# Turned units, early fourth sums, and causal masks added by VectorE, in the hybrid encoder layer on one core

## The chip, the cores and the metric

The kernel runs on one core of a Trainium2 chip. The metric is the time of one execution in device microseconds; several runs of a kernel are taken, and the median counts. Matmuls run on TensorE (PE in the profile, its weight loads PEld) and write to banks of PSUM; VectorE (DVE) and ScalarE (ACT) do the elementwise work; SyncE (SP) and GpSimd (POOL) only issue transfers here.

## The reference

One layer for 512 tokens of width 2048, in float32. A normed input goes through one wide projection into three token mixers of four heads each (width 128), their gates, and three merge gates; the mixers' outputs are projected up, weighted by the gates, summed, projected again and added to the input.

```python
hn = rmsnorm(x, norm_g)
proj = jnp.einsum('bsd,dc->bsc', hn, w_in)     # q, k, v, gate of A, B, C; merge gates
...
# A: logits + c[query] - c[key]; mask = key <= query; softmax; @ v
# B: logits + a bias by relative distance; softmax over the last 9 chunks of 64; @ v
# C: z = q.k * scale; mask = key < query; lk = where(mask, log_sigmoid(-z), 0)
#    a = where(mask, exp(z + sums of lk over later keys), 0); @ v
ys = ys * jax.nn.silu(br[:, :, :, 3])
up = jnp.einsum('bsnw,nwd->bsnd', ys, w_up)
merged = jnp.sum(gates * up, axis=2)
return x + jnp.einsum('bsd,de->bse', merged, w_out)
```

A and C are causal, so their scores need a mask in the 128x128 block on the diagonal of each block of 128 queries.

## The kernel before, in words

**Precision.** Every operand of a large matmul is split into a high part (rounded to the type that TensorE runs fast) and a low part, the rest. ScalarE writes the high part (L245), VectorE subtracts it from the source for the low part (L249). A product is high x high, high x low and low x high. The inputs' two parts lie side by side, 256 tokens each, so that one matmul of 512 columns does weights' high part times both (tile `wh`), and one of 256 columns does weights' low part (tile `wl`) times the inputs' high part.

**Products.** Two columns of 128 outputs each, over a depth of 2048 and two halves of the tokens, are computed by Strassen's scheme with seven products instead of eight (class `PairTask`). A unit (class `Pair`) is one such product: eight matmuls of 512 with `wh` and then eight of 256 with `wl`, into one PSUM bank. The units of a pair come in the order 1, 2, 6, 5, 7, 3, 4; products 6, 7, 3 and 4 go on adding onto the bank of an earlier one (6 onto 1, 7 onto 6, 3 onto 5, 4 onto 7). Sums of weights are made by GpSimd's adding transfers and by VectorE (L631, L637), sums of inputs by `combos`.

**Stages.** First four columns of C's head 0 directly; then, for each of the other heads, its q and k, v and gate as pairs of columns, with the columns of the merge gates between; then the up stage, where for each of 16 blocks of 128 output rows (row block d) three mixers' outputs `y` are multiplied with `w_up` (36 matmuls of 512 columns) and weighted by gates loaded from DRAM into `sg` tiles; then the output projection with `w_out`, again in pairs. `merged_a` and `merged_b` make the sums of inputs that the output's products read: `m1`, `m2`, `m23` (second and third sums) and `m4` (the fourth sums, products 4). Row blocks k and k + 8 make the sums of index k. The fourth sum is written into a tile `mu`, kept, and split into its two parts only when the up stage is over (`late_t4`). The first output pair works in the order 1, 5, 2, 3, 6, 7, 4 with 256-wide matmuls throughout (`late`).

**Attention.** Each head's scores, transposes and value products are spread by `stages` over the units of the next heads. `soft_scores` (A and B) does three matmuls (L259 to L261) for a block of queries i and all keys up to it, then VectorE adds the bias and takes the maximum in one instruction (L986). For A a fourth matmul, the identity times the mask table in bfloat16, adds the mask (L981); `stick_scores` (C) does the same (L1037) before ScalarE copies the scores to `z` (L1042).

**What sets the order.** The program is recorded by a planner, class `Flow`: tasks are generators that yield what they wait for (an event, a number of free buffers in a `Slots` pool) or an engine with an estimated cost, and the one that can start first goes next, by its due time where two can. `stream` walks through the list of units; `at(u, g)` spawns a task when unit u is reached. The order that comes out is fixed on TensorE, ScalarE and VectorE. `t2s` counts the 20 work buffers of 128x512, `atts` four PSUM banks for attention and the up stage, `accs` four for products, `xps` the tiles that hold inputs in two parts, `raws` the buffers for weights as loaded.

Of the kernel before, what the change touches and what calls it, by code (L numbers as in the profile page):

```python
# [15 lines left out]
P = 128  # L16
# [9 lines left out]
UK = 8  # L26
# [122 lines left out]
def mm_us(n, x=1):  # L149
    return x * max(0.115, n / 2400 + 0.0133)  # L150
# [11 lines left out]
def hybrid_kernel(  # L162
# [151 lines left out]
    identb = cp.tile([P, P], BF16, name="identb")  # L314
    nc.vector.tensor_copy(identb, identf)

# [32 lines left out]
    def at(u, g):  # L349
        side.setdefault(u, []).append(g)  # L350

    class Unit:


        def __init__(self, mms, after=None, shape=(UK, P), srcs=()):
            self.shape, self.mms, self.after, self.srcs = list(shape), mms, after, srcs
            self.ready_hi, self.ready, self.there, self.raw = Event(), Event(), Event(), None

# [229 lines left out]
    class PairTask:  # L588
# [57 lines left out]
        def mms_of(self, i):  # L646
            p = self.order[i]
            bank = (0, 1, 2, 0, 0, 1, 2)[i] if self.late else {2: 1, 5: 2, 3: 2}.get(p, 0)
            onto = None if self.late else {6: 1, 7: 6, 4: 7, 3: 5}.get(p)
            more = onto is not None  # L650
            single = self.late or self.plain_end and p == 4
# [3 lines left out]
            def go(u):  # L655
                if more:
# [6 lines left out]
                for j in range(UK):  # L663
                    yield lambda: self.ops[p](j) is not None
                    r, _, ev = self.ops[p](j)
                    yield ev
                    if single:
                        yield PE, mm_us(HS)
                        mm(self.ps[p][:, LH], u.hi[:, j, :], r[:, 0, :], j == 0 and not more, more=more)
                    else:  # L670
                        yield PE, mm_us(S)
                        mm(two(self.ps[p]), u.hi[:, j, :], r, j == 0 and not more, more=more)
                    if single:
                        yield PE, mm_us(HS)
                        mm(self.ps[p][:, LH], u.hi[:, j, :], r[:, 1, :], more=more)
                yield u.ready
                for j in range(UK):
                    yield PE, mm_us(HS)
                    mm(self.ps[p][:, LH], u.lo[:, j, :], self.ops[p](j)[1], stop=j == UK - 1, more=more)
# [191 lines left out]
    class Head:  # L871
# [98 lines left out]
        def soft_scores(self, i):  # L970
# [6 lines left out]
            yield PE, mm_us(m, 3) + (0.05 if n == A else 0)  # L977
# [11 lines left out]
            give(atts)  # L989
            yield ACT, act_us(m) + 0.25  # L990
# [35 lines left out]
        def stick_scores(self, i):  # L1026
# [7 lines left out]
            yield PE, mm_us(m, 3) + 0.05  # L1034
            ps = att()[:, :m]
            mm3(ps, qh[:, blk(i)], ql[:, blk(i)], kh[:, :m], kl[:, :m], True, False)
            nc.tensor.matmul(ps[:, blk(i)], identb, mskc, start=False, stop=True)  # L1037
# [5 lines left out]
            give(atts)  # L1043
            yield t2s, 2
# [89 lines left out]
        def stages(self):  # L1134
# [118 lines left out]
    def schedule(head, a, b):  # L1253
        for (d, g), base in [(g, a) for g in head.stages()[0]] + [(g, b) for g in head.stages()[1]]:
            at(base + d, g)
# [131 lines left out]
    m1, m2, m23, m4 = [None] * UK, [None] * UK, [None] * UK, [None] * (UK // 2)  # L1387
    m4_ev = [Event() for _ in range(UK // 2)]
    kept_m, m1_ev, mus, up_half, up_done = {}, [Event() for _ in range(UK)], {}, Event(), Event()
# [9 lines left out]
    def merged_b(k, b):  # L1399
# [4 lines left out]
        if k % 2 == 0:  # L1404
            yield t2s, 1
            mus[k // 2] = t2("mu")
        u = mus[k // 2][:, RH if k % 2 else LH]
# [11 lines left out]
        minus(u, t[:, LH], b[:, LH])  # L1419
        give(t2s)  # L1420
        ready = up_half if k < 5 else up_done
# [7 lines left out]
        yield up_done  # L1429
        yield from late_t4(k, u, due)  # L1430

    def late_t4(k, u, due):
        if k % 2 == 0:
            yield xps, 1
            m4[k // 2] = Parts("m4")
            set_(m4_ev[k // 2])
        yield m4_ev[k // 2]
        h, lo, ev = m4[k // 2].half(k % 2)
        yield from split(h, lo, u, HS, ev, (due + 14.0,))
        if k % 2:  # L1440
            give(t2s)
# [10 lines left out]
    mops = strassen_ops(m1, m2, m23, m4)  # L1452
# [76 lines left out]
    def stream():  # L1529
        for i, u in enumerate(units):  # L1530
            cur[0] = i
            for g in side.pop(i, ()):
                spawn(g(), 5.0, flow.fin)
# [3 lines left out]
            yield u.ready_hi  # L1537
            yield from u.mms(u)
# [20 lines left out]
KEPT = 1  # L1559
WARM = 16  # L1560
# [59 lines left out]
```

## Time and profile before

| | |
|---|---|
| median of 3 runs | 1327.93 us (1326.29 to 1328.51) |
| the profiled execution | 1328.65 us |
| its span in the trace | 1326.9 us |
| granted TensorE clock | 1.0 |
| busy | PE 1320.2, DVE 1134.7, ACT 805.9, POOL 94.9 us |

A page of the profile has busy time by engine first, the chain of work that ended last in its part 4, and groups of instructions by source line in its part 5. Views of the trace give waits (who waited for whom: us in total, times, longest), windows (busy time by engine in a stretch), and the timeline (start, length, engine, line, operation, tiles written and read, size, count; in brackets idle time of the engine before it and what ended it). Matmuls overlap, so the distance from one start to the next is the time that one holds the array. Many operations are recorded by helpers: L264 is every matmul of a product, L245 and L249 every split.

### The profile page before, as it was taken

The page shows a single profiled execution, that of the slowest core. Times are in us where ns is not written, and L with a number is a line of the kernel's source. Part 1 is how long each engine was busy: PE and PEld are TensorE (multiplying, and loading weights), DVE is VectorE, ACT ScalarE, POOL GpSimd, SP SyncE. Part 2 cuts the span into 40 slices and gives each one's busy share as a digit, 9 for nine tenths or more (in the row PEclk, how much of TensorE's full clock was granted, in tenths as well). Part 3 has the DMA queues.
Part 4 walks back from the last instruction along what each step waited for, and adds up shares of the span by engine and source line. Part 5 has one row for each costly group of instructions (what it writes and reads, how often), then busy time and mean ns, then how long its engine had stood idle before and what let it go on. Part 6 is the DMA issues. An engine that isn't in the chain of part 4 may idle for free.

```text
span 1326.9 us, 20238 instructions
## 1 busy us (share of the span) xinstructions
PE 1320.2 (99%) x7506; PEld 1150.5 (87%) x7506; DVE 1134.7 (86%) x1676; ACT 805.9 (61%) x1280; POOL 94.9 (7%) x120
## 2 busy tenths in 40 slices
PE   9999999999999999999999999999999999999998
PEld 6898888888888888888888888888888888888887
DVE  8989888788888889888898979888898877897786
ACT  8767657575556665666656665666557655454443
POOL 0000001000010100000000000000000000001000
PEclk9999999999999999999999999999999999999999
DMA  9776776767786776867878777776779755668893
GB/s 336 207 206 168 190 198 176 212 177 190 200 203 172 197 201 181 219 160 207 200 182 215 173 193 201 192 196 181 194 178 272 278 194 184 193 172 243 235 254 94
DMA packets 89651, 266.24 MB, mean 201 GB/s; under 512 B 10560, under 2 KB 12608, under 8 KB 89552
## 3 DMA queue, kind: packets, MB, share of 16 engines
q1 hardware_dynamic: 70400, 203.86, 46.4%
q0 software_dynamic: 15552, 56.63, 25.8%
q10 hardware_dynamic: 3600, 4.46, 0.9%
q8 instruction: 59, 0.97, 0.3%
q14 instruction: 40, 0.33, 0.1%
HBM read 245.21 MB, written 19.70 MB: 200 GB/s over the span
## 4 chain that ended last, share of the span: by engine, by line
PE 98%; DVE 1%; DMA 0%; issue 0%; DVEq 0%
PE acc L264 84%; PE att L264 8%; PE att L1008 1%; PE att L259 1%; PE att L260 1%; PE att L1121 1%; PE att L1122 1%; PE att L261 1%; PE att L1120 1%; PE att L1072 0%; PE att L1222 0%; DMA begin_in<-in_begin 0%; PE att L909 0%; PE att L910 0%; DVE m L249 0%; DVE wl L249 0%
## 5 line engine op out<-in xcount | busy, mean ns | idle before, releaser
L249 DVE TENSOR_TENSOR wl<-raw,wh 128x1024 fp32r<-128x1024 f32 (+2 forms) x418 | 499.8, 1199 | 141.9 <-ACT wh L245 133.6
L245 ACT ACTIVATE wh<-raw 128x1024 fp32r<-128x1024 f32 (+2 forms) x418 | 434.1, 1039 | 145.3 <-PE acc L264 62.3
L264 PE MATMUL acc<-x,wh 128*128 128x512 f32 (+1 forms) x1568 | 399.2, 391 | 0.7 <-DVE gq L333 0.7
L264 PEld LDWEIGHTS acc<-x,wh 128*128 128x128 f32 x1568 | 277.3, 189 | 50.1 <-issue 2.2
L264 PE MATMUL acc<-t,wh 128*128 128x512 f32 (+1 forms) x1128 | 283.7, 390 | 0.0
L264 PEld LDWEIGHTS acc<-t,wh 128*128 128x128 f32 x1128 | 198.1, 189 | 32.9
L264 PEld LDWEIGHTS acc<-x,wl 128*128 128x128 f32 x1504 | 207.0, 190 | 17.2 <-DVE x L441 0.8
L264 PE MATMUL acc<-x,wl 128*128 128x256 f32 (+1 forms) x1504 | 216.8, 285 | 0.0
L264 PEld LDWEIGHTS acc<-t,wl 128*128 128x128 f32 x1104 | 151.6, 190 | 11.4
L264 PE MATMUL acc<-t,wl 128*128 128x256 f32 x1104 | 155.5, 282 | 0.0
L282 POOL DMA_DIRECT2D raw<-in_w_col x92 | 79.5, 864 | 924.1 <-DMA raw<-in_w_col 573.8
L264 PE MATMUL acc<-m,wh 128*128 128x512 f32 (+1 forms) x512 | 113.7, 366 | 1.5 <-DVE m L249 1.5
L264 PEld LDWEIGHTS acc<-m,wh 128*128 128x128 f32 x512 | 85.4, 190 | 14.4 <-DVE m L249 1.9
L815 ACT ACTIVATE c<-acc 128x256 f32<-128x256 f32 x51 | 19.6, 383 | 97.1 <-PE acc L264 94.1
L782 ACT ACTIVATE u<-acc 128x512 f32<-128x512 f32 x51 | 30.3, 594 | 79.4 <-PE acc L264 79.4
L761 ACT ACTIVATE u<-acc 128x512 f32<-128x512 f32 x52 | 31.1, 598 | 71.9 <-PE acc L264 70.8
L637 DVE TENSOR_TENSOR raw<-raw,raw 128x1024 f32<-128x1024 f32 x54 | 65.9, 1220 | 0.5
L631 DVE TENSOR_TENSOR raw<-raw,raw 128x1024 f32<-128x1024 f32 x54 | 65.8, 1219 | 0.4
L264 PE MATMUL att<-y,wh 128*128 128x512 f32 x256 | 65.8, 389 | 0.0
L264 PEld LDWEIGHTS acc<-m,wl 128*128 128x128 f32 x448 | 60.6, 191 | 3.7
L264 PE MATMUL acc<-m,wl 128*128 128x256 f32 x448 | 62.5, 282 | 0.0
L264 PEld LDWEIGHTS att<-y,wh 128*128 128x128 f32 x256 | 48.0, 188 | 10.0
(207 smaller groups left out, 1397.2 us busy)
## 6 DMA issues: line engine op xcount, KB each, us to landing
raw<-in_w_col SPq DMA_DIRECT2D x230, 512.0 KB, 4.5
raw<-in_w_col POOLq DMA_DIRECT2D x92, 512.0 KB, 6.4
raw<-in_w_out SPq DMA_DIRECT2D x40, 512.0 KB, 5.3
gl<-c SPq DMA_DIRECT2D x48, 256.0 KB, 3.5
raw<-in_w_up SPq DMA_DIRECT2D x32, 384.0 KB, 3.6
sg<-gl SPq DMA_DIRECT2D x48, 256.0 KB, 4.8
raw<-in_w_out POOLq DMA_DIRECT2D x16, 512.0 KB, 6.9
xn<-in_xn SPq DMA_DIRECT2D x16, 256.0 KB, 3.1
```

The costliest lines, as they stand in the source:

```text
L245: nc.scalar.activation(hi, src, AF.Copy)
L249: nc.vector.tensor_sub(lo, src, f(hi))
L259: nc.tensor.matmul(ps, lh, rh, start=start, stop=False, skip_group_check=more)
L260: nc.tensor.matmul(ps, lh, rl, start=False, stop=False, skip_group_check=more)
L261: nc.tensor.matmul(ps, ll, rh, start=False, stop=stop, skip_group_check=more)
L264: nc.tensor.matmul(ps, w, x, start=start, stop=stop, skip_group_check=more)
L282: nc.gpsimd.dma_start(to, src, accum_op=ALU.add)
L631: nc.vector.tensor_add(w[1], w[1], w[5])
L637: nc.vector.tensor_add(w[2], w[2], w[1])
L761: nc.scalar.activation(self.u, ps, AF.Copy)
L782: nc.scalar.activation(self.s, ps, AF.Copy)
L815: nc.scalar.activation(c, ps[:, RH], AF.Copy, scale=-1.0)
```

## The change

It has four parts. **Turned units:** a `Pair` that adds onto an earlier product's bank may run its low-part matmuls first and its high-part ones after; `stream` turns it when the unit before ended with low parts and the planner has its low part ready 0.4 us ahead. **Masks:** the matmuls with the mask tables go. For A, VectorE adds the mask into the diagonal block of the bias tile, in place; as a later block of queries needs that stretch of the bias without a mask, the blocks go from the last to the first, and the addition of block i waits for the maximum of block i + 1 (event "m"). For C, VectorE adds the mask to `z` after ScalarE's copy. **Fourth sums:** they are written into the upper half of `b`, split at once in the up stage, and kept in tiles `m4` out of the 20 work buffers `t2s` instead of in four tiles of `xps`; `m23` may take its tile one index earlier (k < 6). **Due times:** the sums of weights are due 1.5 us after they can start instead of 3, the last head's stages 3 instead of 5.

```diff
     class Pair(Unit):
+            self.single = task.late or task.plain_end and self.p == 4
+            self.onto = None if task.late else {6: 1, 7: 6, 4: 7, 3: 5}.get(self.p)
...
-                spawn(self.task.sums(), 3.0)
+                spawn(self.task.sums(), 1.5)
...
+                def high(first):
+                    for j in range(UK):
...
+                            mm(two(self.ps[p]), u.hi[:, j, :], r, start, stop, more)
+                def low(first):
+                    yield u.ready
+                    for j in range(UK):
...
+                        mm(self.ps[p][:, LH], u.lo[:, j, :], x, first and j == 0 and not more,
+                           not first and j == UK - 1, more)
+                steps = (low, high) if u.low_first else (high, low)
+                for first, step in zip((True, False), steps):
+                    yield from step(first)
...
     def soft_scores(self, i):
-            mm3(ps, qh[:, blk(i)], ql[:, blk(i)], kh[:, :m], kl[:, :m], True, n == B)
+            mm3(ps, qh[:, blk(i)], ql[:, blk(i)], kh[:, :m], kl[:, :m], True, True)
+            p = self.p[i]
             if n == A:
-                nc.tensor.matmul(ps[:, blk(i)], identb, mska, start=False, stop=True)
-            p = self.p[i]
+                if i < QB - 1:
+                    yield self.event("m", i + 1)
+                yield DVE, dve_us(P)
+                nc.vector.tensor_add(self.bias[:, blk(i)], self.bias[:, blk(i)], mska)
...
+            set_(self.event("m", i))
...
     def stick_scores(self, i):
-            mm3(ps, qh[:, blk(i)], ql[:, blk(i)], kh[:, :m], kl[:, :m], True, False)
-            nc.tensor.matmul(ps[:, blk(i)], identb, mskc, start=False, stop=True)
+            mm3(ps, qh[:, blk(i)], ql[:, blk(i)], kh[:, :m], kl[:, :m], True, True)
...
+            yield DVE, dve_us(P)
+            nc.vector.tensor_add(z[:, blk(i)], z[:, blk(i)], mskc)
...
-                g += [(s + i, one(self.soft_scores, i)) for i in range(QB)]
+                g += [(s + i, one(self.soft_scores, QB - 1 - i if self.n == A else i)) for i in range(QB)]
...
     def merged_b(k, b):
-        minus(u, t[:, LH], b[:, LH])
+        minus(b[:, RH], t[:, LH], b[:, LH])
+        yield t2s, 1
+        parts, ev = t2("m4", F32R), Event()
+        yield from split(parts[:, LH], parts[:, RH], b[:, RH], HS, ev)
         give(t2s)
-        ready = up_half if k < 5 else up_done
+        m4[k] = two(parts), parts[:, LH], ev
+        ready = up_half if k < 6 else up_done
...
-        yield up_done
-        yield from late_t4(k, u, due)
-
-    def late_t4(k, u, due):
...
     def stream():
+            if isinstance(u, Pair) and not u.single:
+                low_there = u.ready.t is not None and u.ready.t + AHEAD <= flow.clock[PE]
+                u.low_first = ends_low and u.onto is not None and low_there
+                ends_low = not u.low_first
+            else:
+                ends_low = False
...
+AHEAD = 0.4
```

Where instructions move, first on TensorE, at the third and fourth unit of a pair while a head of B is under way (`acc_4250` and `acc_4198` before are `acc_4248` and `acc_4195` in the changed kernel; `x` and `t` are inputs and their sums). Before:

```order
L264 MATMUL acc_4250<-x_17_130,wh_4173 128x512
L264 MATMUL acc_4250<-x_10_123,wl_4174 128x256
...
L264 MATMUL acc_4250<-x_17_130,wl_4174 128x256
L264 MATMUL acc_4198<-t_67_387,wh_4196 128x512
...
L264 MATMUL acc_4198<-t_102_644,wh_4196 128x512
L264 MATMUL acc_4198<-t_67_387,wl_4197 128x256
...
L264 MATMUL acc_4198<-t_102_644,wl_4197 128x256
L264 MATMUL acc_4314<-x_2_115,wh_4248 128x512
```

In the changed kernel:

```order
L264 MATMUL acc_4248<-x_17_128,wh_4171 128x512
L264 MATMUL acc_4248<-x_10_121,wl_4172 128x256
...
L264 MATMUL acc_4248<-x_17_128,wl_4172 128x256
L264 MATMUL acc_4195<-t_67_385,wl_4194 128x256
...
L264 MATMUL acc_4195<-t_102_642,wl_4194 128x256
L264 MATMUL acc_4195<-t_67_385,wh_4193 128x512
...
L264 MATMUL acc_4195<-t_102_642,wh_4193 128x512
L264 MATMUL acc_4312<-x_2_113,wh_4246 128x512
```

The eight `wl` matmuls of the later unit moved ahead of its eight `wh` ones, so two narrow runs stand together and then two wide ones. This is so in 136 units.

On VectorE, at the scores of A's first head (`cb` is the bias, `mx` the maxima). Before:

```order
L986 ISA p_7598,mx_7690<-att_7685,cb_7521 128x128
L988 TENSOR_SCALAR mx_7690<-mx_7690 128x1
L249 TENSOR_TENSOR wl_7663<-raw_7526,wh_7662 128x1024
L986 ISA p_7599,mx_7697<-att_7692,cb_7521 128x256
L988 TENSOR_SCALAR mx_7697<-mx_7697 128x1
...
L249 TENSOR_TENSOR wl_7720<-raw_7413,wh_7719 128x1024
```

In the changed kernel:

```order
L995 TENSOR_TENSOR cb_7519<-cb_7519,mska 128x128
L999 ISA p_7595,mx_7727<-att_7695,cb_7519 128x512
L1001 TENSOR_SCALAR mx_7727<-mx_7727 128x1
L779 TENSOR_TENSOR u_7683<-u_7683,acc_7686 128x512
L711 TENSOR_TENSOR c_1366_7744<-u_7683 128x256
L249 TENSOR_TENSOR wl_7736<-raw_7568,wh_7735 128x1024
L995 TENSOR_TENSOR cb_7519<-cb_7519,mska 128x128
...
L999 ISA p_7596,mx_7766<-att_7701,cb_7519 128x384
L1001 TENSOR_SCALAR mx_7766<-mx_7766 128x1
```

An addition into the bias stands ahead of each block's maximum, the widest block comes first, and low parts stand between.

On VectorE, at the first output pair (the numbers of `m23` tell its tiles apart). Before:

```order
L717 TENSOR_TENSOR c1_2181_12063<-u_2170_11987,acc_2178_12027 128x256
L249 TENSOR_TENSOR wl_2177_12026<-raw_2120_11720,wh_2176_12025 128x1024
L249 TENSOR_TENSOR m23_2157_11911<-mt_2082_11535,m23_2157_11911 128x2x256
L249 TENSOR_TENSOR m23_2163_11946<-mt_2110_11677,m23_2163_11946 128x2x256
L249 TENSOR_TENSOR m23_2164_11947<-mt_2137_11818,m23_2164_11947 128x2x256
L722 TENSOR_TENSOR c1_2181_12063<-c2_2175_12024,acc_2184_12066 128x256
L249 TENSOR_TENSOR m23_2174_12010<-mt_2166_11963,m23_2174_12010 128x2x256
...
L249 TENSOR_TENSOR m4_2165_11949<-mu_1973_10970,m4_2165_11949 128x256 x2
```

In the changed kernel:

```order
L249 TENSOR_TENSOR m4_2180_12057<-sg_2134_11807,m4_2180_12057 128x256
L727 TENSOR_TENSOR c1_2182_12073<-u_2170_11997,acc_2179_12036 128x256
L249 TENSOR_TENSOR wl_2172_11999<-raw_2127_11764,wh_2171_11998 128x1024
L249 TENSOR_TENSOR m23_2158_11921<-mt_2056_11399,m23_2158_11921 128x2x256
L249 TENSOR_TENSOR m23_2159_11922<-mt_2084_11543,m23_2159_11922 128x2x256
L249 TENSOR_TENSOR m23_2160_11923<-mt_2112_11687,m23_2160_11923 128x2x256
L249 TENSOR_TENSOR m23_2167_11959<-mt_2138_11827,m23_2167_11959 128x2x256
L732 TENSOR_TENSOR c1_2182_12073<-c2_2176_12033,acc_2185_12076 128x256
L249 TENSOR_TENSOR m23_2186_12081<-mt_2174_12017,m23_2186_12081 128x2x256
```

The last fourth sum's split moved ahead of product 2's sum, the eight after it are gone, and four splits of `m23` instead of three stand behind the low part.

More of the change, by code (lines that the diff above doesn't have):

```diff
@@ L655, in go @@
             def go(u):
+                single, onto = u.single, u.onto
+                more = onto is not None
                 if more:
@@ L661, in go @@
                     self.ps[p] = acc(bank)
[L663 to L667, printed above, removed]
-                        yield PE, mm_us(HS)
[L669 to L679, printed above, removed]
+                def high(first):
+                    for j in range(UK):
+                        yield lambda: self.ops[p](j) is not None
+                        r, _, ev = self.ops[p](j)
+                        yield ev
+                        start, stop = first and j == 0 and not more, not first and j == UK - 1
+                        if single:
+                            yield PE, mm_us(HS)
+                            mm(self.ps[p][:, LH], u.hi[:, j, :], r[:, 0, :], start, stop, more)
+                            yield PE, mm_us(HS)
+                            mm(self.ps[p][:, LH], u.hi[:, j, :], r[:, 1, :], more=more)
+                        else:
+                            yield PE, mm_us(S)
+                            mm(two(self.ps[p]), u.hi[:, j, :], r, start, stop, more)
@@ L1254, in schedule @@
         for (d, g), base in [(g, a) for g in head.stages()[0]] + [(g, b) for g in head.stages()[1]]:
-            at(base + d, g)
+            at(base + d, g, 3.0 if head.last else 5.0)
     def first_head(n, h):
```

44 lines of the change are left out of this document (16 added, 28 removed).

## The prediction

> **What bounds the kernel now.** I read the first page, then the waits of TensorE, then its timeline, and VectorE's rows last.
>
> ```profile
> span 1326.9 us, 20238 instructions
> PE 1320.2 (99%) x7506; PEld 1150.5 (87%) x7506; DVE 1134.7 (86%) x1676; ACT 805.9 (61%) x1280; POOL 94.9 (7%) x120
> PE 98%; DVE 1%; DMA 0%; issue 0%; DVEq 0%
> PE acc L264 <- DVE m L249: 1.5, 2, 1.3
> ```
>
> TensorE is busy for 99% of the span and makes up 98% of the chain that ended last; its only wait of any size is the last row, 1.5 us in two pieces. A change pays here if TensorE issues fewer matmuls, issues them closer together, or loses that wait; it costs if TensorE has to wait for something new. So the first question is how far apart matmuls start, in the middle of the kernel:
>
> ```profile
> 600.35 2.00 PE L264 MATMUL acc<-t,wh 128*128 128x512 f32 x8
> 602.19 1.11 PE L264 MATMUL acc<-t,wl 128*128 128x256 f32 x8
> 603.14 2.00 PE L264 MATMUL acc<-x,wh 128*128 128x512 f32 x8
> ...
> 608.73 2.00 PE L264 MATMUL acc<-x,wh 128*128 128x512 f32 x8
> ```
>
> Columns: start, length, what. Lengths overlap, so I use starts. A unit is eight 512-wide matmuls with the weights' high part and eight 256-wide ones with the low part: 1.84 us and 0.95 us, and over three units 8.38/3 = 2.793 us. Where runs of one width stand behind each other, in the up stage and at the first output pair, the same widths take:
>
> ```profile
> 1161.14 1.98 PE L264 MATMUL att<-y,wh 128*128 128x512 f32 x8
> 1162.95 1.07 PE L264 MATMUL att<-y,wl 128*128 128x512 f32 x4
> ...
> 1166.73 2.08 PE L264 MATMUL acc<-m,wh 128*128 128x256 f32 x16
> 1168.65 1.12 PE L264 MATMUL acc<-m,wl 128*128 128x256 f32 x8
> 1169.61 2.08 PE L264 MATMUL acc<-m,wh 128*128 128x256 f32 x16
> ```
>
> Eight of 512 behind 512 take 1.81 us, and 256-wide ones behind 256 take 1.92/16 = 0.96/8 = 0.12 us each. Going from a narrow run to a wide one therefore costs 1.84 - 1.81 = 0.03 us; going from wide to narrow gives back 0.96 - 0.95 = 0.01.
>
> **Turned units.** No matmul is removed; 136 units run low part first (counted in the changed order, first place shown in the section on the change), and each takes one narrow-to-wide passage away. A turned unit costs 1.81 + 0.96 = 2.77 us instead of 2.793: by the runs 0.02 us, by the three-unit mean 0.023. 136 x 0.02 = 2.7 us (2.0 to 3.1, the rows being rounded to 0.01).
>
> The price is a wait: a turned unit needs its low part at its start, 1.84 us earlier. If VectorE is late, everything behind it on TensorE is late too. Of the 136 units, in this trace, 130 had their low part written at least 1 us before their start; the six others had 0.31 (once) to 0.93 us. The smallest, and one of the four at 0.87:
>
> ```profile
> 1028.95 1.22 DVE L249 TENSOR_TENSOR wl<-raw,wh 128x1024 fp32r<-128x1024 f32 x1
> ...
> 421.58 1.22 DVE L249 TENSOR_TENSOR wl<-raw,wh 128x1024 fp32r<-128x1024 f32 x1
> ```
>
> ```profile
> 1030.48 2.00 PE L264 MATMUL acc<-t,wh 128*128 128x512 f32 x8
> ...
> 423.67 0.63 PE L264 MATMUL acc<-t,wh 128*128 128x512 f32 x2
> ```
>
> 1030.48 - (1028.95 + 1.22) = 0.31; 423.67 - 422.80 = 0.87. I take no wait, and keep up to 3 us for the upper end: the six units at half a us each.
>
> **Masks.** Removed: 32 mask matmuls and their weight loads. A head of A (four blocks, each with a mask) against a head of B (the same four blocks, none):
>
> ```profile
> 821.03 0.22 PE L259 MATMUL att<-qkh,qkh 128*128 128x128 f32 x1
> ...
> 823.32 0.36 PE L264 MATMUL acc<-x,wl 128*128 128x256 f32 x1
> 823.52 0.85 PE L264 MATMUL acc<-x,wh 128*128 128x512 f32 x3
> ```
>
> ```profile
> 395.02 0.22 PE L259 MATMUL att<-qkh,qkh 128*128 128x128 f32 x1
> ...
> 396.94 0.85 PE L264 MATMUL acc<-x,wh 128*128 128x512 f32 x3
> ```
>
> 2.29 us against 1.92, and the matmul behind the last mask holds the array for 0.20 us where 0.12 is its own: 0.37 + 0.08 = 0.45 us a head, 1.8 us for four. In C each mask stands alone:
>
> ```profile
> 286.94 0.23 PE L1037 MATMUL att<-mskc,identb 128*128 128x128 bf16 x1
> 286.98 1.40 PE L264 MATMUL acc<-x,wh 128*128 128x512 f32 x5
> 288.22 1.12 PE L264 MATMUL acc<-x,wl 128*128 128x256 f32 x8
> ```
>
> 0.04 us itself, and five wide ones behind it take 1.24 us where 5 x 1.84/8 = 1.15 is usual: 0.13 us, 2.1 us for sixteen (1.8 by A's 0.11). Together I take 3.7 us, from 3.6 to 3.9.
>
> Two thirds of that is not the mask's own time but a stretched neighbour. The Trainium skill, "TensorE: Matmul & The Clock Gate", section "Back-to-back issue gap", would speak against this change: it gives a matmul's spacing as its columns at 2.4 GHz plus about 2.5 ns, whatever stands before it; by that a mask costs an estimated 56 ns and turning saves nothing, so the sum would lose 1.8 us instead of 6.4 in these two parts. The rows disagree: 1.84 and 1.81 us for the same eight, 0.20 and 0.12 for the same one.
>
> Added on VectorE: 32 additions of 128x128. Nearest row, and the idle time that covers them:
>
> ```profile
> L249 DVE TENSOR_TENSOR al<-att,ah 128x128 fp32r<-128x128 f32 x12 | 3.4, 283 | 0.0
> 60.00:380.00 320.00, 320.00 (x1909) 282.54 (x1908) 274.47 (x379) 205.14 (x332) 25.84 (x30) 1.00 0.72 188
> 720.00:1045.00 325.00, 325.00 (x1879) 284.91 (x1878) 287.83 (x433) 205.19 (x326) 23.30 (x27) 1.00 0.77 208
> DVE wl L249 <- ACT wh L245: 133.6, 112, 2.1
> ```
>
> (Windows: length, then busy us of TensorE, its loads, VectorE, ScalarE, GpSimd.) 32 x 0.283 = 9.1 us, half in C's stage, half in A's, where VectorE is idle for 45.5 and 37.2 us, mostly waiting for a high part of ScalarE. So I cost them at nothing; uncovered they cost 9.1. In A a block's addition now waits for the reduction of the block before it, and its own reduction for the addition; behind them on VectorE stand low parts, and the scores keep their PSUM bank meanwhile. The next to want one in that head, the transposes, are planned six units of 2.79 us later, so this too I take at nothing, with up to 1 us a head inside the 3 us of waits. In C, ScalarE's |z| waits for the addition, with high parts behind it. The cast to `identb` at the start goes, under the wait for the first input. The earlier weight sums (due 1.5 us after they are ready, not 3) move additions only, ahead of other VectorE work; uncovered, one costs its 1.22 us. SP's and GpSimd's queues keep their order but for the gate loads (below).
>
> **Fourth sums.** The only real wait stands in the last unit of the first output pair:
>
> ```profile
> 1181.13 1.08 PE L264 MATMUL acc<-m,wh 128*128 128x256 f32 x7
> 1182.38 0.84 PE L264 MATMUL acc<-m,wh 128*128 128x256 f32 x4 [0.16 <-DVE m L249]
> 1184.52 1.05 PE L264 MATMUL acc<-m,wh 128*128 128x256 f32 x5 [1.30 <-DVE m L249]
> 1185.41 1.11 PE L264 MATMUL acc<-m,wl 128*128 128x256 f32 x8
> ```
>
> Sixteen matmuls take 4.28 us instead of 16 x 0.12 = 1.92: 2.36 us, which go, as all eight fourth sums are split in the up stage. What is late next is product 6, two units earlier, which reads the second and third sums `m23`:
>
> ```profile
> 1173.03 1.22 DVE L249 TENSOR_TENSOR wl<-raw,wh 128x1024 fp32r<-128x1024 f32 x1
> 1174.16 1.89 DVE L249 TENSOR_TENSOR m<-mt,m 128x512 fp32r<-128x512 f32 x3
> 1175.97 0.42 DVE L722 TENSOR_TENSOR c<-c,acc 128x256 f32<-128x256 f32 x1
> 1176.30 0.68 DVE L249 TENSOR_TENSOR m<-mt,m 128x512 fp32r<-128x512 f32 x1
> ```
>
> ```profile
> 1175.37 2.08 PE L264 MATMUL acc<-m,wh 128*128 128x256 f32 x16
> ```
>
> The last `m23` is done at 1176.98 and needed by the 15th matmul at 1175.37 + 14 x 0.12 = 1177.05: 0.07 us to spare. In the changed order four splits instead of three stand between this low part and that addition, (1175.97 - 1174.16)/3 = 0.60 us more, so TensorE waits 0.53 us there (0 to 1.3). Net 2.36 - 0.53 = 1.8 us.
>
> **The sum.** 2.7 + 3.7 + 1.8 = 8.2 us. The profiled execution took 1328.65 us, 1.75 more than its span, which this leaves; 1328.65 - 8.2 = 1320.4. It lay 0.72 above the median of the three runs, so against that median: 1327.93 - 8.2 = 1319.7 us.
>
> **Rivals.** (1) *A matmul's spacing is its own*, as in the rule above. Then the masks bring 32 x 0.04 = 1.3 us, turning nothing, the sums 1.8: 1324.8 us. Both pairs of rows speak against it. Chance 0.05. (2) *The additions land on TensorE's path*: VectorE becomes the bound in A's and C's heads, and the 9.1 us eat the 8.2: 1328.8 us, no change. It decides from where VectorE has no idle time left in a head; the 45.5 and 37.2 us speak against it. Chance 0.06. (3) *Slower: late gates in the up stage.* The eight fourth sums now keep eight of the twenty work buffers that gate loads draw on too, and their loads are issued later, singly, between weight loads.
>
> ```profile
> sg<-gl SPq DMA_DIRECT2D x48, 256.0 KB, 4.8
> L1331 ACT ACTIVATE sg<-sg,begin_in 128x512 f32<-128x512 f32 x48 | 32.1, 709 | 0.0
> ```
>
> If the three loads of a row block come one behind the other, each waiting for a buffer, a block takes 3 x 4.8 + 0.71 = 15.1 us against its 36 matmuls of 1.81/8 us, 8.15; with the last two blocks so, 13.9 us are lost: 1333.6 us. It decides where fewer than three buffers are free at a block's end. Against it: in the changed order some twenty VectorE instructions stand between the one that frees a late gate's buffer and the one that uses it. Chance 0.06. That the change does not do what it says I leave no chance: the order shows it.
>
> **How the numbers follow.** My case has 0.83. Its best end is 3.1 + 3.9 + 2.4 = 9.4 us, and 1.3 more of the 1.64 us by which the lowest of the three runs lies under their median: 1317.2. Its worst is 2.0 + 3.6 + 1.1 less 3.0 of waits, 3.7 us: 1324.2, which I round to 1324.0. That is the range; it leaves out the rivals, 0.17. About 0.2% (2.7 us) is what a measurement of this kernel can tell from no change. My case is faster by more; rival 1 for two thirds; rival 2 is the same, with a third of rival 1; rival 3 is slower: 0.86, 0.08, 0.06.
>
> **What would show it.** After: no mask matmul between L261 and the next matmul; narrow runs of sixteen, with the wide run behind them the only one at 1.84; in the last unit of the first output pair sixteen matmuls in 1.92 us, and in product 6 a wait of about half a us for `m`; VectorE busy some 9 us longer. Wrong: waits of TensorE for `wl` that add up to more than 3 us (turned units too early), waits for a bank or for `sg` in the up stage (rival 3), or wide runs at 1.84 behind wide runs (rival 1).

## The result, and the profile after

The changed kernel takes 1319.7 us (median of 6 runs, 1318.54 to 1320.77) where the kernel before takes 1327.76 us (6 runs, 1326.29 to 1328.51): a ratio of 0.994, 95% interval 0.9928 to 0.9953. Forecast were 1319.7 us. The profiled execution took 1318.54 us, the shortest of its six.

The first page of the changed kernel, its parts 1 and 4:

```profile
span 1316.8 us, 20264 instructions
PE 1311.3 (100%) x7474; PEld 1149.1 (87%) x7474; DVE 1140.6 (87%) x1707; ACT 807.2 (61%) x1280; POOL 95.0 (7%) x120
PE 99%; DVE 1%; DMA 0%; ACT 0%; issue 0%; ACTq 0%
```

TensorE has 32 matmuls fewer (7474 for 7506) and is still the bound. Its waits, all of them:

```profile
PE att L1553 <- POOL tmpc L307: 1.1, 1, 1.1
PE acc L264 <- DVE gq L330: 0.7, 1, 0.7
PE acc L264 <- DVE m L249: 0.3, 1, 0.3
```

The first two lie in the first 6 us and were there before. Of the 1.5 us for `m` 0.3 are left. Two turned units in the timeline of TensorE, in the middle of the kernel:

```profile
600.60 1.12 PE L264 MATMUL acc<-t,wl 128*128 128x256 f32 x8
601.56 2.00 PE L264 MATMUL acc<-t,wh 128*128 128x512 f32 x8
603.40 1.98 PE L264 MATMUL acc<-x,wh 128*128 128x512 f32 x8
605.21 1.11 PE L264 MATMUL acc<-x,wl 128*128 128x256 f32 x8
606.17 2.00 PE L264 MATMUL acc<-x,wh 128*128 128x512 f32 x8
```

The wide run behind a narrow one takes 1.84 us (601.56 to 603.40), the wide run behind that one 1.81. A head of A's scores now ends without masks:

```profile
816.07 0.39 PE L259 MATMUL att<-qkh,qkh 128*128 128x512 f32 x1
...
817.92 0.91 PE L264 MATMUL acc<-x,wh 128*128 128x512 f32 x3
```

They take 1.85 us instead of 2.29 (by 0.07 less than the 1.92 of a head of B, whose blocks go from narrow to wide). The first output pair, products 6, 7 and 4:

```profile
1167.43 1.96 PE L264 MATMUL acc<-m,wh 128*128 128x256 f32 x15
1169.71 0.38 PE L264 MATMUL acc<-m,wh 128*128 128x256 f32 x1 [0.32 <-DVE m L249]
1169.93 1.11 PE L264 MATMUL acc<-m,wl 128*128 128x256 f32 x8
1170.88 2.08 PE L264 MATMUL acc<-m,wh 128*128 128x256 f32 x16
...
1173.77 2.08 PE L264 MATMUL acc<-m,wh 128*128 128x256 f32 x16
1175.68 1.12 PE L264 MATMUL acc<-m,wl 128*128 128x256 f32 x8
```

Product 4's sixteen matmuls take 1.91 us instead of 4.28; product 6's take 2.50 (1167.43 to 1169.93) where 1.92 is usual. And VectorE's new additions, from its groups by line:

```profile
L995 DVE TENSOR_TENSOR cb<-cb,mska 128x128 f32<-128x128 f32 x16 | 4.5, 282 | 0.0
L1058 DVE TENSOR_TENSOR z<-z,mskc 128x128 f32<-128x128 f32 x16 | 4.3, 283 | 0.0
```

No wait of TensorE names them.

**Where the time went, stage by stage.** Both kernels have the same units, counted here as 0 to 418 by their weight tiles on TensorE. The table gives, for some units, the start in the trace of before (us), and in the other rows how much later (+) or earlier (-) the unit starts than before, both counted from the start of unit 1, so that the first 8 to 10 us drop out. C's heads are over by unit 112, B's by 224, A's stage reaches to unit 330, the up stage is units 331 to 362, the first output pair 363 to 369; the columns 364 and 371 each stand one product behind the start of a pair. The column of 308 lies ahead of the last head of A. Each row is one profiled execution; "alone" is the kernel before with one part of the change. These kernels are told of below.

| start of unit | 112 | 224 | 308 | 336 | 364 | 371 | 418 |
|---|---|---|---|---|---|---|---|
| before | 369.88 | 708.23 | 963.20 | 1053.70 | 1166.73 | 1189.15 | 1320.44 |
| changed | -2.52 | -3.37 | -5.23 | -5.88 | -5.88 | -7.54 | -7.89 |
| masks alone | -1.90 | -1.90 | -3.28 | +1.53 | +1.54 | +1.54 | +1.54 |
| turned units alone | -0.73 | -1.36 | -1.84 | -2.09 | -2.09 | -0.55 | -0.95 |
| fourth sums alone | -0.03 | -0.03 | -0.03 | -0.03 | -0.03 | -1.69 | -0.31 |
| due times alone | -0.01 | -0.14 | -0.10 | -0.06 | -0.06 | -0.29 | -0.29 |
| masks and due times | -2.03 | -2.15 | -3.55 | -4.01 | -4.01 | -4.24 | -4.24 |
| changed, no due times | -2.68 | -3.32 | -5.22 | -2.21 | -2.21 | -3.85 | -2.82 |
| changed, sums due after 3 | -2.67 | -3.31 | -5.20 | -4.15 | -4.15 | -5.50 | -4.47 |
| changed, other order of products | -2.67 | -3.51 | -5.38 | -6.03 | -6.03 | -8.25 | -6.94 |
| changed, that order and earlier sums | -2.66 | -3.51 | -5.37 | -6.02 | -6.02 | -7.49 | -7.85 |
| changed, turned units alternating | -0.55 | +0.63 | +0.53 | +0.48 | +0.48 | -1.17 | -0.32 |

The changed kernel gains in the heads of C and A (masks and turned units), in B (turned units), nothing in the up stage, 1.66 us in the first output pair and 0.35 in the later ones. The four parts alone end at +1.54, -0.95, -0.31 and -0.29, together -0.01; the whole ends at -7.89. That gap is what the experiments are about.

What the table leaves out is the start. The first product matmuls of the two profiled executions, before and then changed:

```profile
5.42 1.19 PE L264 MATMUL acc<-x,wh 128*128 128x512 f32 x2 [0.69 <-DVE gq L333]
6.41 1.05 PE L264 MATMUL att<-x,wh 128*128 128x512 f32 x2
```

```profile
5.31 0.70 PE L264 MATMUL acc<-x,wh 128*128 128x512 f32 x2 [0.70 <-DVE gq L330]
5.86 0.62 PE L264 MATMUL att<-x,wh 128*128 128x512 f32 x2
```

Two matmuls of 512 take 0.85 us in one and 0.46 in the other. The start makes 2.18 us of the 10.1 between the two spans. What speaks for its coming and going with one and the same kernel stands in the last section; the table leaves it out.

### The profile page after: what moved, and what is told of

It is laid out like the page before. It is cut to its first block, busy times and chain, and to the rows that moved or that the text cites. A ratio compares the mean times of both kernels' runs of the same rounds, so it can differ in the third digit from the quotient of the medians.

```text
span 1316.8 us, 20264 instructions
## 1 busy us (share of the span) xinstructions
PE 1311.3 (100%) x7474; PEld 1149.1 (87%) x7474; DVE 1140.6 (87%) x1707; ACT 807.2 (61%) x1280; POOL 95.0 (7%) x120
## 3 DMA queue, kind: packets, MB, share of 16 engines
q1 hardware_dynamic: 70400, 203.86, 45.5%
## 4 chain that ended last, share of the span: by engine, by line
PE 99%; DVE 1%; DMA 0%; ACT 0%; issue 0%; ACTq 0%
PE acc L264 85%; PE att L264 8%; PE att L1022 1%; PE att L260 1%; PE att L1136 1%; PE att L261 1%; PE att L1137 1%; PE att L259 1%; PE att L1135 1%; PE att L1087 0%; PE att L1237 0%; PE att L919 0%; PE att L920 0%; DMA begin_in<-in_begin 0%; DVE m L249 0%; DVE wl L249 0%
## 5 line engine op out<-in xcount | busy, mean ns | idle before, releaser
L264 PEld LDWEIGHTS acc<-x,wh 128*128 128x128 f32 x1568 | 283.7, 188 | 56.1 <-issue 2.2
L264 PE MATMUL acc<-t,wh 128*128 128x512 f32 (+1 forms) x1128 | 280.3, 388 | 0.0
L264 PEld LDWEIGHTS acc<-t,wl 128*128 128x128 f32 x1104 | 144.7, 191 | 2.1
L264 PE MATMUL acc<-m,wh 128*128 128x512 f32 (+1 forms) x512 | 109.7, 364 | 0.3 <-DVE m L249 0.3
L264 PE MATMUL acc<-m,wl 128*128 128x256 f32 x448 | 59.8, 283 | 0.0
```

Of the source, the lines that this page charges most:

```text
L264: nc.tensor.matmul(ps, w, x, start=start, stop=stop, skip_group_check=more)
```

## The experiments

**Masks alone.** The kernel before, with both mask parts of the change.

```diff
-                nc.tensor.matmul(ps[:, blk(i)], identb, mska, start=False, stop=True)
+                nc.vector.tensor_add(self.bias[:, blk(i)], self.bias[:, blk(i)], mska)
...
-            nc.tensor.matmul(ps[:, blk(i)], identb, mskc, start=False, stop=True)
+            nc.vector.tensor_add(z[:, blk(i)], z[:, blk(i)], mskc)
```

> The kernel before with only the masks moved to VectorE (A's blocks last to first, additions into the bias and into z); units are not turned, fourth sums stay late. If a mask costs its own 0.04 us and stretches the matmul behind it: 3.7 us less, about 1324.0 us; the array's holds behind the score matmuls read 0.12 us for 256 columns and 0.23 for 512, and the wait for the fourth sums stays at 2.4 us. If a matmul's spacing is its own: 1.3 us less, about 1326.4. If VectorE's 32 additions lie on TensorE's path: 9.1 - 3.7 us more, about 1333, with waits of TensorE for wl or for a PSUM bank in the heads of A and C.

Measured: 1330.15 us, ratio to before 1.0019 (1.001 to 1.0028): slower. Yet by unit 322, the last ahead of the up stage that can be compared, it is 3.72 us early, 1.90 in C and 1.82 in A, where 3.7 were forecast. All of it and more is lost where the last head of A meets the up stage. Its timeline of TensorE there:

```profile
1027.61 2.00 PE L264 MATMUL acc<-y,wh 128*128 128x512 f32 x8
...
1034.44 0.39 PE L1122 MATMUL att<-ah,vh 128*128 128x512 f32 x1
1036.03 0.50 PE L1123 MATMUL att<-ah,vl 128*128 128x512 f32 x1 [1.21 <-DVE vl L1084]
...
1039.38 0.49 PE L264 MATMUL att<-y,wh 128*128 128x512 f32 x1 [1.44 <-ACT y L245]
...
1041.84 3.09 PE L264 MATMUL acc<-y,wh 128*128 128x512 f32 x8
1044.77 1.09 PE L264 MATMUL acc<-y,wl 128*128 128x512 f32 x4
```

The value products (L1122 to L1124) of the last head stand 6.83 us behind the start of the up stage; in the kernel before they came ahead of it. TensorE waits there for the low part `vl`, then for the head's own output `y`, and the next eight wide matmuls take 2.93 us instead of 1.81. So masks on VectorE are a gain in every head, and all of it is lost where the last head hands over.

**Turned units alone.** The kernel before, with the turned units, the same 136.

```diff
+                u.low_first = ends_low and u.onto is not None and low_there
...
+                steps = (low, high) if u.low_first else (high, low)
```

> The kernel before with only the turned units (136 of them); masks stay on TensorE, fourth sums stay late. If the passage from a narrow to a wide run costs 0.03 us and the way back gives 0.01: 136 x 0.02 = 2.5 to 2.7 us less, about 1325.2 us, with wide runs behind wide ones at 1.81 us and the others still at 1.84. If a matmul's spacing is its own: no change, 1327.8. If turned units wait for their low parts: the same or slower, with waits of TensorE for wl.

Measured: 1325.84 us, ratio 0.9981 (0.9972 to 0.999). Up to the first output pair 2.09 us are gained and in the later pairs 0.40, 2.5 in all. The 1.5 us that the table loses between 364 and 371 come behind the old wait for the fourth sums:

```profile
1182.17 1.06 PE L264 MATMUL acc<-m,wh 128*128 128x256 f32 x5 [1.30 <-DVE m L249]
1183.06 1.58 PE L264 MATMUL acc<-m,wl 128*128 128x256 f32 x8
1184.44 3.12 PE L264 MATMUL acc<-m,wh 128*128 128x512 f32 x8
1187.40 1.11 PE L264 MATMUL acc<-m,wl 128*128 128x256 f32 x8
```

Eight narrow in 1.38 us and eight wide in 2.96, with nothing to wait for: the granted clock is 0.59 from 1184.4 to 1187.4 us, in this execution.

**Fourth sums alone.**

```diff
-        minus(u, t[:, LH], b[:, LH])
+        minus(b[:, RH], t[:, LH], b[:, LH])
+        parts, ev = t2("m4", F32R), Event()
+        yield from split(parts[:, LH], parts[:, RH], b[:, RH], HS, ev)
```

> The kernel before with only the early fourth sums. The 2.36 us of wait in the last unit of the first output pair go, and product 6 waits about 0.5 us for the last m23, as VectorE's order there is that of the changed kernel: 1.8 us less, about 1326.0 us. If late gates in the up stage decide (eight of the twenty work buffers held): slower than before, with waits of TensorE for a PSUM bank between 1100 and 1165 us of the span.

Measured: 1328.09 us, ratio 0.9997 (0.9988 to 1.0006): the same, not the 1.8 us less that were expected. In the trace nothing happens ahead of product 6, 0.69 us is lost there, 2.35 is won in product 4, and then 1.38 goes again in the last output pair, where TensorE waits for weights (0.44 us for `wh`, 0.40 for `wl`). The up stage loses nothing, so the rival of late gates falls.

**The mask's type.** The kernel before, with identity and mask tables in the type of the matmuls around them instead of bfloat16.

```diff
-    identb = cp.tile([P, P], BF16, name="identb")
+    identb = cp.tile([P, P], F32R, name="identb")
```

> The kernel before with identity and mask tables in float32r, the type of all other matmuls, instead of bfloat16; the 32 mask matmuls stay. Tells what stretches the matmul behind a mask. If it is the change of type: the mask itself takes about 0.11 us (as the other 128-wide matmuls do) and the 512-wide one behind it 0.23 instead of 0.32, so a mask costs about as much as before, 1327.5 us. If it is the narrowness of the mask: the mask takes 0.11 us and the matmul behind it stays at 0.32, 32 x 0.07 = 2.2 us more, 1330 us.

Measured: 1328.75 us, ratio 1.0004 (0.9995 to 1.0013). One mask of C:

```profile
286.92 0.22 PE L1037 MATMUL att<-mskc,identb 128*128 128x128 f32 x1
286.98 1.37 PE L264 MATMUL acc<-x,wh 128*128 128x512 f32 x5
288.19 1.11 PE L264 MATMUL acc<-x,wl 128*128 128x256 f32 x8
```

The mask holds the array 0.06 us and the five behind it 1.21, together 1.27; in bfloat16 it was 0.04 and 1.24, together 1.28. The mask itself takes 0.06 us, not the 0.11 that both cases expected, but the sum stays, and unit 418 starts only 0.23 us later than before: the stretched neighbour is not a price of changing the type.

**Masks with the due times.** As the first, and the last head's stages due after 3, the sums after 1.5.

```diff
-                spawn(self.task.sums(), 3.0)
+                spawn(self.task.sums(), 1.5)
...
-            at(base + d, g)
+            at(base + d, g, 3.0 if head.last else 5.0)
```

> The kernel before, with the masks on VectorE and the due times (sums of weights 1.5, the last head's stages 3), no turned unit, fourth sums late. Theory (the masks are worth 3.7 us in the heads, and masks alone lost 5.3 us only because the planner put the last head's transposes and value products so late that they fell into the up stage; with its stages due after 3 they stand about five units ahead of it): the gain survives, 1324.1 us (1323.3 to 1325.0), and TensorE shows no wait for y or vl around 1035 us. Rival (the additions themselves make the last head late, whatever its due time): 1328.5 to 1330.5 us, with the same waits.

Measured: 1323.81 us, ratio 0.997 (0.996 to 0.9981). The gain survives: -3.98 at unit 322, -4.01 behind the hand-over. The value products now stand 12.6 us ahead of the up stage:

```profile
1014.67 0.39 PE L1122 MATMUL att<-ah,vh 128*128 128x512 f32 x1
...
1027.29 2.00 PE L264 MATMUL acc<-y,wh 128*128 128x512 f32 x8
```

The rival, that the additions make the last head late whatever its due time, falls.

**The changed kernel without the due times.** The same two edits undone in the changed kernel.

> The changed kernel with the due times as before (sums 3, all stages 5); turned units, masks and early fourth sums stay. Theory (the due times keep the last head and the output's weight sums from being late): the last head's value products now stand behind the first block of the up stage instead of five units ahead of it, so part of what masks alone lost there comes back, 1 to 4 us, and some of the 1.4 us in the later output pairs: 1323 us (1320.7 to 1325.5). Rival (due times cost and bring nothing, as the prediction had it): 1319.7 us (1319.0 to 1320.4).

Measured: 1325.88 us (1322.43 to 1326.25), ratio 0.9982 (0.9973 to 0.9991), a little above the range expected; the rival, that they bring nothing, falls. At the hand-over 3.7 us go:

```profile
1025.58 1.98 PE L264 MATMUL acc<-y,wh 128*128 128x512 f32 x8
...
1028.30 0.39 PE L1135 MATMUL att<-ah,vh 128*128 128x512 f32 x1
...
1035.21 0.50 PE L264 MATMUL att<-y,wh 128*128 128x512 f32 x1 [0.76 <-ACT y L245]
1036.48 0.50 PE L264 MATMUL att<-y,wh 128*128 128x512 f32 x1 [0.77 <-DVE y L249]
...
1037.85 3.45 PE L264 MATMUL acc<-y,wh 128*128 128x512 f32 x8
1041.14 1.09 PE L264 MATMUL acc<-y,wl 128*128 128x512 f32 x4
```

The value products stand 2.7 us behind the start of the up stage instead of 12.6 ahead, TensorE waits for `y` twice, and then issues eight wide matmuls in 3.29 us instead of 1.81. In the last output pair 1.33 us go (-4.15 at unit 406), as with the fourth sums alone. The three of the eleven runs with a mean granted clock of 1.0 took 1322.43 to 1322.74 us, the other eight, at 0.999, 1323.96 to 1326.25: the eight slow matmuls, which make 1.5 us of the trace's loss, most likely do not come in every execution.

**Only the sums due after 3.**

> The changed kernel with only the sums of weights due after 3 as before; the last head's stages stay at 3. Theory (the two due times serve two places: the head's the hand-over to the up stage, the sums' the last output pair): no loss at the hand-over, and the waits of TensorE for wh and wl in the last output pair, 1.4 us: 1321.1 us (1320.4 to 1322.0). Rival (only the last head's due time counts): 1319.7 us.

Measured: 1324.08 us (1321.86 to 1324.29), ratio 0.9967 (0.9956 to 0.9979), above the range expected. The 1.3 us in the last pair are there (-5.80 at unit 406, -4.47 at 418), and no wait at the hand-over. But 1.7 us more than expected go in A's last head. The two rows of the waits, and where the longest one is:

```profile
PE acc L264 <- DVE wl L249: 1.7, 2, 1.3
...
PE acc L264 <- ACT wh L245: 0.5, 1, 0.5
```

```profile
967.12 2.06 PE L264 MATMUL acc<-t,wh 128*128 128x512 f32 x8
970.50 1.22 PE L264 MATMUL acc<-t,wl 128*128 128x256 f32 x8 [1.31 <-DVE wl L249]
```

VectorE writes a low part too late for a unit that is not even turned. With both due times undone, in the kernel above, this wait is not there (-5.76 at unit 322 against the changed kernel's -5.74): it comes where the last head's stages are due earlier and the sums are not. The two due times thus serve three places, and the sums' one is worth 3.4 us in this kernel (-7.89 against -4.47), more than expected.

**The due times alone.**

> The kernel before with the due times alone. Theory (the due times gain nothing by themselves; they only keep the other parts from being late): 1327.5 us (1326.8 to 1328.2), the same as before. Rival (they are worth some us by themselves, and a part of the whole's 8 us is theirs): 1324 to 1326 us.

Measured: 1326.65 us, ratio 0.9996 (0.9987 to 1.0005): the same, and 0.29 us less in the table, though the median lies 0.15 us under the range expected. They gain next to nothing; they keep the rest from losing.

**Another order in the first output pair.** Product 4 ahead of 6 and 7, as its sums are ready and theirs are not.

```diff
+            if late == 2:
+                self.order = (1, 5, 2, 3, 4, 6, 7)
```

> The changed kernel with the first output pair's products in the order 1, 5, 2, 3, 4, 6, 7, so that the product of the fourth sums, which are ready, stands before the two that need the last m23. Theory (the 0.58 us wait in product 6 is one of order alone): it goes, 1319.1 us (1318.5 to 1319.7). Rival (VectorE is behind as a whole at this place, and the wait moves to another product): 1319.7 us or up to 1 us more.

Measured: 1321.3 us (1320.02 to 1321.75), ratio 0.9955 (0.9941 to 0.9969). The wait is gone, 0.71 us at unit 371. But in the last pair 1.57 go (-8.51 at unit 406). VectorE's sum of weights and what waits for it, in the changed kernel and then here:

```profile
1293.86 1.22 DVE L631 TENSOR_TENSOR raw<-raw,raw 128x1024 f32<-128x1024 f32 x1
```

```profile
1295.89 1.22 DVE L633 TENSOR_TENSOR raw<-raw,raw 128x1024 f32<-128x1024 f32 x1
...
1299.98 2.14 PE L264 MATMUL acc<-m,wh 128*128 128x512 f32 x8 [0.71 <-ACT wh L245]
...
1302.49 1.21 PE L264 MATMUL acc<-m,wl 128*128 128x256 f32 x8 [0.37 <-DVE wl L249]
```

The same sum stands 2 us later, behind a split and an addition that it was ahead of. Neither theory had that.

**That order, with earlier sums from the up stage on.**

```diff
-                spawn(self.task.sums(), 1.5)
+                spawn(self.task.sums(), 0.5 if cur[0] >= 340 else 1.5)
```

> The changed kernel with the order 1, 5, 2, 3, 4, 6, 7 in the first output pair and, of the units reached in the up stage and after it, the sums of weights due 0.5 us after they can start instead of 1.5, which puts the last pair's first sum two splits and a half earlier on VectorE, where the changed kernel has it. Theory (the order alone gained 0.7 us at the first output pair and gave 1.6 back in the last pair, because that sum stood later): both are kept, 1319.0 us (1318.2 to 1319.9). Rival (the wait for weights in the last pair comes wherever TensorE arrives there earlier): 1321 us.

Measured: 1319.23 us (1318.97 to 1321.13), ratio 0.9941 (0.9929 to 0.9954). The last pair waits no more, but a sum now stands ahead of the splits of the first pair, and a wait for `m` is back, now in the third product of the pair:

```profile
1164.40 0.39 PE L264 MATMUL acc<-m,wh 128*128 128x256 f32 x1 [0.62 <-DVE m L249]
```

At unit 418 it is 0.04 us from the changed kernel. The median fits what was expected, the mechanism doesn't.

**And a longer warm-up.**

```diff
-WARM = 16
+WARM = 19
```

> As the kernel before this one in the list, with 19 instead of 16 matmuls of the warm-up ahead of the first real one, which fills TensorE's idle 0.4 to 1.2 us there. Theory (that pause is what lets the first eight or so real matmuls run at half the clock, 0.43 us each, in some executions and not in others): the slow starts become rare, and the median is 0.5 to 1.5 us lower than without, 1318 us. Rival (the half clock at the start has nothing to do with the pause): the same median within 0.4 us.

Measured: 1319.13 us (1318.94 to 1319.45), ratio 0.9936 (0.9922 to 0.9949). The median is that of the kernel without it. All five runs are at the low end, where two of the other's five took 1320.87 and 1321.13; five runs are too few to call that an effect. In the trace unit 418 starts at -7.86, as without it. Neither of the last two is shown to beat the changed kernel.

**Turned units that alternate.** The changed kernel, with the matmuls of a turned unit in the order low, high, low, high.

```diff
+                        mm(self.ps[p][:, LH], u.lo[:, j, :], x, more=more)
+                        yield PE, mm_us(S)
+                        mm(two(self.ps[p]), u.hi[:, j, :], r, False, j == UK - 1, more)
```

> The changed kernel with the low and the high matmuls of each turned unit one by one in turn (256, 512, 256, 512, ...) instead of eight and eight; the same matmuls and operands. Theory (each passage from narrow to wide costs 27 ns and each from wide to narrow gives back 8, whoever stands there): seven more pairs of passages a unit, 7 x 0.019 = 0.13 us, times 136 is 18 us: 1338 us (1334 to 1342). Rival (a matmul's spacing is its own, and turning gained by something else, such as an earlier release of the weight tiles): 1319.7 us (1319 to 1321).

Measured: 1326.62 us (1325.89 to 1328.68), ratio 0.9996 (0.9987 to 1.0005): 6.9 us more than the changed kernel between the medians and 7.6 by the table, where 18 and 0 were expected.

```profile
604.58 0.28 PE L264 MATMUL acc<-t,wl 128*128 128x256 f32 x1
604.70 0.40 PE L264 MATMUL acc<-t,wh 128*128 128x512 f32 x1
604.93 0.28 PE L264 MATMUL acc<-t,wl 128*128 128x256 f32 x1
605.05 0.40 PE L264 MATMUL acc<-t,wh 128*128 128x512 f32 x1
```

By the medians over some 930 such pairs a narrow one holds the array 118 ns here and a wide one 236, against 120 and 227 in runs of their own width: 7 ns a pair, and 7 x 8 x 136 makes the 7.6 us. In the changed kernel the first five wide ones behind a narrow run take 233, 236, 228, 232 and 231 ns instead of 227, and the first narrow one behind a wide run 114 instead of 120 (means). So the 27 ns of a passage are spread over five matmuls; where the width changes at each, only a part falls due each time. The spacing depends on what stands before, which the rival denied; that each passage costs the same holds for runs of eight or sixteen alone.

## Why the prediction was right, point by point

**Turned units**: 2.7 us forecast (2.0 to 3.1); alone they gave 2.5 in the trace and 2.6 between the medians. The term was sized from rows rounded to 0.01. By the means of the runs a turned unit makes one wide run 1814 ns instead of 1841 and one narrow run 960 instead of 952: 19 ns, 136 x 0.019 = 2.6 us. No turned unit waited, as forecast. The rival by which a matmul's spacing is its own falls with this and with the alternating kernel; the runs show 227 to 236 ns for one and the same matmul. The section of the Trainium skill that it leaned on ("TensorE: Matmul & The Clock Gate", "Back-to-back issue gap") gives its formula for the isolated matmul, about 216 ns at 512 columns, and 131 ns in a sustained stream; neither is what these runs show.

**Masks**: 3.7 us forecast, 3.72 by unit 322 with masks alone, 1.90 of it in C (2.1 by the term) and 1.82 in A (1.8). That two thirds of it is a stretched neighbour is borne out, as 32 masks of 0.04 us make 1.3 us of it; that the change of type makes the stretch was not claimed, and isn't so.

**The additions on VectorE**: costed at nothing, since VectorE was idle for 45.5 and 37.2 us in these stages. In the changed kernel that holds: no wait of TensorE names them. But the reason was too weak. Masks alone had the same idle time and lost 5.3 us (from -3.72 to +1.54) at the last head, whose output the up stage needs at once. Idle time does not tell the two cases apart: in the 33 us up to 1027 us VectorE is idle for 2.3 us with masks alone, and for 2.6 us with masks and due times, where nothing is lost. What differs is the place of the head's last instructions in the recorded order. The loss that the prediction's second rival expected from the additions does come at this one place, but only where the due times are missing, and not because VectorE has no idle time left, which is the reason it gives. VectorE's busy time grew by 5.9 us where "some 9" were named; the two groups of additions do add up to 8.8.

**Due times**: this is the step that failed, without showing in the sum. The text gave the sums' due time one sentence ("move additions only") and the last head's none. By the table they are worth 5.1 us of the 7.9 (-7.89 against -2.82), 1.5 of them by the eight slow matmuls, and by the two ratios to before, which hold the start too, 5.6 (0.9982 against 0.994): without them the last head's value products fall into the up stage and weights come late in the last output pair; with the sums' one alone undone, weights come late in A's last head too. The forecast of the whole was right because it was made against the order of the changed kernel, in which these waits are already averted, and not because each part is harmless.

**Fourth sums**: 2.36 - 0.53 = 1.8 us forecast, 1.66 in the changed kernel and 1.66 alone (-0.03 to -1.69). Product 4's wait went whole; the new one in product 6 cost 0.69 by the starts of units (0.58 in its sixteen high-part matmuls, 0.11 ahead of them), not 0.53. That view of waits which shows 0.3 counts only the idle time of the last matmul.

**The sum**: 8.2 us forecast, 7.89 in the trace from unit 1 on, 8.06 between the medians. That all three terms came out within 0.2 us is what bears the forecast; that the two medians agree to 0.1 us is luck, as the changed kernel's six runs alone lie 2.2 us apart.

## What to carry to other kernels

Idle time of an engine in a stage does not by itself show that added work is covered: look at the last tile of the stage and at what the next stage needs first, and see in the order where that stands. When several edits meet in one change, run each alone and the whole without each (here only the due times were taken out of the whole): the parts add up to nothing and the whole gains 8 us, and without the edit that looked like bookkeeping 5 of them are lost. A wait is sized by the distance between starts, not by the idle time that the waits list.

## What the runs showed of the hardware

**Half clock behind short waits.** After waits of 1.21 and 1.44 us within 5 us (masks alone), of 0.76 and 0.77 (no due times) and of 1.30 (turned units alone) the next eight wide matmuls took 2.93, 3.29 and 2.96 us, where 1.81 to 1.84 is usual, with no wait among them. The clock that these traces record stood at half for 3.41 us, from 1040.79, 1037.56 and 1183.44 us on (0.60, 0.52 and 0.59 over the eight matmuls). So a wait can cost up to another 3.41/2 = 1.7 us behind itself. All three stretches begin a whole number of 3.413 us after the full clock was first granted in their trace (302, 301 and 344 times, from 9.96, 10.15 and 9.25 us on). What makes the clock fall stays open: in the kernel before the same wait of 1.30 us was followed by eight narrow matmuls at their usual length, and in masks alone, too, the wait of 1.30 us for `m` has no half clock behind it. The Trainium skill, "TensorE: Matmul & The Clock Gate", "Part 1: The HAM clock gate (the "warmup" mystery)", lets the clock fall after some 3.4 us of idleness; these waits are shorter.

**The start.** How long the first matmuls run at half clock differs: the full clock is recorded from 9.93 us on in the kernel before and from 4.36 in the changed one, and of the first matmuls of 512, ten take 0.43 us or more in the one and none in the other, with none to ten in the other traces. Only one execution of each kernel was traced; that this differs between executions of one kernel is read from its times, which lie in two groups: the kernel with the due times alone took 1326.38 to 1326.65 us in six runs and 1327.65 to 1328.63 in five. The pause ahead of the first matmul doesn't decide it: 0.69 us in the start at half clock shown above, 0.70 in the other. The same section of the Trainium skill says that the number of such matmuls varies from run to run. The traces of these kernels, not of one kernel, agree. For a comparison below 0.2%, count from the first product on.

**Widths.** A matmul of 512 columns in a run of its own width takes 226.7 ns, one of 256 takes 120; that a narrow run makes the next five wide ones slower, and a 128-wide mask in either type the five behind it by 0.06 to 0.09 us, had no explanation in any view, and none is offered.
